# Loading the first tile in two DMAs of every other partition

## The chip, the core and the metric

The kernel runs on one core of one Trainium2 chip. The metric is the device time of one execution in microseconds (us). VectorE, ScalarE and GpSimd compute, SyncE only issues DMAs, and 16 DMA engines move the data between HBM and the core's on-chip memory of 128 partitions. TensorE is not used.

## What is computed

A mixture-of-experts combine. For each of 16 x 1024 tokens there are two expert rows of 512 float32 values and two weights; the output is the weighted sum of the two rows.

```python
weights = combine_weights[..., np.newaxis]
return np.sum(expert_outputs * weights, axis=2).astype(np.float32)
```

A token comes in as 4,096 bytes (two rows of 2,048) and goes out as 2,048. In all 67.2 MB are read and 33.6 MB written.

## The kernel before, in words

The 16,384 tokens are laid over the 128 partitions, 128 tokens to a partition. The first 115 tokens of a partition are neighbours in HBM, and the last 13 of each are taken from the end of the array (`rows`, L45). So a tile of 13 tokens is, for each partition, one contiguous row of 13 x 4,096 = 53,248 bytes ("52 KB").

There are ten tiles of 12 or 13 tokens (`TILES`, L32). They pass through four rooms in one buffer `et` (`ROOM`, `SITE`, L29 to L31): tile g uses room g modulo 4, so a room can be loaded again only when the output of the tile before in it has been stored. The results are written over the inputs, into the first half of the room, and stored from there.

Work on a tile (`combine`, L81): for tiles 0 to 7 VectorE multiplies the whole tile by the weights, spread along the rows (L88), and adds the two halves (L97). In tile 8, ScalarE shares the multiplications (L92, L94, L96). Tile 9 goes token by token, ScalarE multiplying (L102) and VectorE multiplying and adding (L103). All weights lie in one buffer `wt`.

The order is written out by hand (`manual_schedule`, from L107):

- ScalarE's queue (q10 in the profile) first issues a small store of a zero tile, 16 rows of 512 bytes (L111, overwritten later), then the weights of the first nine tiles, 128 rows of 920 bytes (L79), then the weights of the last tile in two halves of 64 partitions, rows of 104 bytes (L114). Later it issues the stores of tiles 0 to 6 (L130).
- SyncE's queue (q1) issues the loads of the first four tiles (L76). The first tile is loaded as 2 tokens, and these in packets of 4,096 bytes (`max_dma_last_dim`), and then 11 tokens in rows of 45,056 bytes (`FIRST`, L33). Each later load waits for the store that frees its room. The last two stores, tiles 7 and 8 together and tile 9, go out on this queue as well (L130).

There are nine DMAs before the first result: four on ScalarE's queue and five on SyncE's. The fifth load, that of tile 3, also waits until the small store of L111 has landed.

Of the kernel before, what the change touches and what calls it, by code (L numbers as in the profile page):

```python
# [1 line left out]

# [4 lines left out]


@with_exitstack
def kernel(  # L10
    ctx: ExitStack,
    tc: tile.TileContext,
    expert_outputs: bass.AP,
    combine_weights: bass.AP,
    out: bass.AP,
):

    nc = tc.nc
    b, s, k, h = expert_outputs.shape
    assert k == 2
    n = b * s
    P = nc.NUM_PARTITIONS
    per = n // P
    assert per * P == n

    ROOM = [13, 13, 12, 13]  # L29
    ROOMS = len(ROOM)  # L30
    SITE = [sum(ROOM[:i]) for i in range(ROOMS)]  # L31
    TILES = [13, 13, 12, 13, 13, 13, 12, 13, 13, 13]  # L32
    FIRST = [2, 11, 13, 12, 13]  # L33
    STORES = [[0], [1], [2], [3], [4], [5], [6], [7, 8], [9]]
    WHOLE = [0, 1, 2, 3, 4, 5, 6, 7]
    MIXED = [8]
    ALONE = 3
    FREE = {9: 0}
    LAST = 13
    assert all(c <= ROOM[g % ROOMS] for g, c in enumerate(TILES))  # L40
    assert sum(TILES) == per and [g for st in STORES for g in st] == list(range(len(TILES)))
    main = per - LAST
    starts = [sum(TILES[:g]) for g in range(len(TILES))]

    def rows(x):  # L45

        first = x[0 : P * main, :].rearrange("(p t) f -> p t f", p=P)
        second = x[P * main : n, :].rearrange("(p t) f -> p t f", p=P)
        return lambda t, c: first[:, t : t + c, :] if t < main else second[:, t - main : t - main + c, :]

    flat = out.rearrange("b s h -> (b s) h")
    eo = rows(expert_outputs.rearrange("b s k h -> (b s) (k h)"))
    cw = rows(combine_weights.rearrange("b s k -> (b s) k"))
    o = rows(flat)

    dt = mybir.dt.float32
    mult = mybir.AluOpType.mult
    add = mybir.AluOpType.add
    copy = mybir.ActivationFunctionType.Copy

    pool = ctx.enter_context(tc.tile_pool(name="all", bufs=1))
    et = pool.tile([P, sum(ROOM), k * h], dt)
    halves = et.rearrange("p j (k h) -> p (j k) h", k=k)
    wt = pool.tile([P, per * k], dt)
    wk = wt.rearrange("p (t k) -> p t k", k=k)
    zt = pool.tile([16, 128], dt)
    warm = pool.tile([P, 1], dt)

    def place(t):
        g = max(g for g in range(len(TILES)) if starts[g] <= t)  # L70
        return SITE[g % ROOMS] + t - starts[g]

    def load(t, c, **kw):
        at = place(t)
        assert place(t + c - 1) == at + c - 1
        nc.sync.dma_start(out=et[:, at : at + c], in_=eo(t, c), **kw)  # L76

    def weights(q, t, c):
        q.dma_start(out=wk[:, t : t + c, :], in_=cw(t, c))  # L79

    def combine(g, base):  # L81
        at, c, t0 = SITE[g % ROOMS], TILES[g], starts[g]
        if g in WHOLE or g in MIXED:
            room = halves[:, k * at : k * (at + c), :]
            x0, x1 = et[:, at : at + c, 0:h], et[:, at : at + c, h : 2 * h]
            if g in WHOLE:
                wb = wt[:, k * t0 : k * (t0 + c)].unsqueeze(2).to_broadcast([P, k * c, h])
                nc.vector.tensor_tensor(out=room, in0=room, in1=wb, op=mult)  # L88
            else:
                for i in range(ALONE, c):  # L90
                    x = et[:, at + i, 0:h]
                    nc.scalar.activation(out=x, in_=x, func=copy, scale=wt[:, k * (t0 + i) : k * (t0 + i) + 1])  # L92
                w1 = wk[:, t0 : t0 + c, 1:2].to_broadcast([P, c, h])
                nc.vector.tensor_tensor(out=x1, in0=x1, in1=w1, op=mult)  # L94
                w0 = wk[:, t0 : t0 + ALONE, 0:1].to_broadcast([P, ALONE, h])
                nc.vector.tensor_tensor(out=x0[:, 0:ALONE], in0=x0[:, 0:ALONE], in1=w0, op=mult)  # L96
            nc.vector.tensor_tensor(out=halves[:, base : base + c, :], in0=x0, in1=x1, op=add)  # L97
            return
        for i in range(c):
            t = k * (t0 + i)  # L100
            x0, x1 = halves[:, k * (at + i), :], halves[:, k * (at + i) + 1, :]
            nc.scalar.activation(out=x0, in_=x0, func=copy, scale=wt[:, t : t + 1])  # L102
            nc.vector.scalar_tensor_tensor(  # L103
                out=halves[:, base + i, :], in0=x1, scalar=wt[:, t + 1 : t + 2], in1=x0, op0=mult, op1=add
            )

    with tc.manual_schedule():  # L107
        nc.vector.memset(zt, 0.0)  # L108

        ahead = flat[0 : P * main, :].rearrange("(q t) h -> q (t h)", q=16)  # L110
        nc.scalar.dma_start(out=ahead[:, 0:128], in_=zt)  # L111
        weights(nc.scalar, 0, main)
        for half in (slice(0, P // 2), slice(P // 2, P)):
            nc.scalar.dma_start(out=wk[half, main:per, :], in_=cw(main, per - main)[half])  # L114
        nc.scalar.activation(out=warm, in_=nc.const_aps.tensor(1.0, (P, 1), dt), func=copy)  # L115

        t = 0
        for i, c in enumerate(FIRST):
            load(t, c, **({"max_dma_last_dim": k * h * 4} if i == 0 else {}))
            t += c  # L120
        assert t == sum(TILES[:ROOMS])
        for j, st in enumerate(STORES):
            room = FREE.get(st[0], st[0] % ROOMS)
            base, c = SITE[room] * k, 0
            for g in st:
                combine(g, base + c)
                c += TILES[g]
            assert c <= k * ROOM[room]
            q = nc.sync if j in (7, 8) else nc.scalar
            q.dma_start(out=o(starts[st[0]], c), in_=halves[:, base : base + c, :])  # L130
            for g in st:
                if g + ROOMS < len(TILES):
                    load(starts[g + ROOMS], TILES[g + ROOMS])


# [1 line left out]
_INS = ['expert_outputs', 'combine_weights']  # L137
_OUTS = [((16, 1024, 512), 'float32')]


# [23 lines left out]
```

## Time and profile before

| what | value |
|---|---|
| time, median of 3 runs | 238.83 us (238.82 to 238.92) |
| span of the profiled execution, first to last instruction | 237.1 us |
| time of the profiled execution itself | not recorded beside its span |
| VectorE busy | 190.0 us, 80% |
| ScalarE busy | 15.8 us, 7% |
| read from HBM, written to it | 67.24 MB, 33.56 MB |
| rate over the span | 425 GB/s |

The span counts from the first to the last instruction of one execution; the time also holds what lies before and after. A DMA queue's row gives packets, MB and the time that its packets took as a share of 16 engines over the span or window. "Landing" is the moment when a transfer's completion is signalled. A row of the timeline has start, duration, engine, line and operation, and in brackets the idle time before it with what ended it. In the chain of waits, each step is what released the next.

### The profile page before, as it was taken

What the parts mean: (1) busy time and instruction counts of PE and PEld (TensorE: products, weight loads), DVE (VectorE), ACT (ScalarE), POOL (GpSimd) and SP (SyncE); (2) the same over time, 40 slices, a digit from 0 to 9 for tenths busy, and PEclk for the clock granted to TensorE, in tenths of its full rate; (3) what the DMA queues carried; (4) which work ended last, traced back from release to release, by engine and by line L of the source; (5) the groups of instructions that cost most, each with busy time, mean ns of one, the idle gap of its engine ahead of it and who ended that gap; (6) DMA issues with size and microseconds to landing.
All of it is one profiled execution on the core that took longest, in us unless ns stands there. A gap on an engine that the chain in (4) does not pass through costs nothing.

```text
span 237.1 us, 154 instructions
## 1 busy us (share of the span) xinstructions
DVE 190.0 (80%) x33; ACT 15.8 (7%) x25; POOL 0.2 (0%) x4
## 2 busy tenths in 40 slices
DVE  0006999999999999999999998998499969919400
ACT  2000000000000000000000000000000055019200
POOL 0000000000000000000000000000000000000000
DMA  8999999989999999999899999999899999899996
GB/s 300 388 481 434 432 421 398 470 348 485 449 431 458 431 440 390 486 420 420 359 492 409 409 509 392 431 503 431 359 431 503 420 397 483 381 431 431 431 431 287
DMA packets 3344, 100.80 MB, mean 425 GB/s; under 512 B 512, under 2 KB 656, under 8 KB 912
## 3 DMA queue, kind: packets, MB, share of 16 engines
q1 hardware_dynamic: 2000, 77.33, 75.9%
q10 hardware_dynamic: 1344, 23.47, 23.0%
HBM read 67.24 MB, written 33.56 MB: 425 GB/s over the span
## 4 chain that ended last, share of the span: by engine, by line
DVE 55%; DMA 36%; issue 1%; ACT 0%; DVEq 0%; ACTq 0%; SPq 0%
DVE et L88 35%; DVE et L97 17%; DMA out_dram<-et 17%; DMA et<-in_expert_outputs_dram 12%; DMA wt<-in_combine_weights_dram 8%; DVE et L103 3%; ACT et L102 0%; DVEq L159 0%; ACTq L111 0%; DVE zt L108 0%; DVEq L88 0%; SPq L76 0%; ACTq L102 0%
## 5 line engine op out<-in xcount | busy, mean ns | idle before, releaser
L88 DVE TENSOR_TENSOR et<-et,wt 128x13312 f32<-128x13312 f32 (+1 forms) x8 | 110.0, 13754 | 23.8 <-DMA wt<-in_combine_weights_dram 18.7
L97 DVE TENSOR_TENSOR et<-et 128x6656 f32<-128x6656 f32 (+1 forms) x9 | 62.8, 6973 | 0.4
L92 ACT ACTIVATE et<-et,wt 128x512 f32<-128x512 f32 x10 | 6.2, 708 | 188.0 <-DMA et<-in_expert_outputs_dram 188.0
L103 DVE SCALAR_TENSOR_TENSOR et<-et,wt 128x512 f32<-128x512 f32 x13 | 8.7, 747 | 5.0 <-ACT et L102 5.0
L102 ACT ACTIVATE et<-et,wt 128x512 f32<-128x512 f32 x13 | 8.1, 707 | 14.0 <-DMA et<-in_expert_outputs_dram 14.0
L94 DVE TENSOR_TENSOR et<-et,wt 128x6656 f32<-128x6656 f32 x1 | 7.1, 7093 | 2.3 <-DMA et<-in_expert_outputs_dram 2.3
L96 DVE TENSOR_TENSOR et<-et,wt 128x1536 f32<-128x1536 f32 x1 | 1.8, 1751 | 0.0
L115 ACT ACT_TABLE_LOAD x1 | 1.3, 1283 | 3.1 <-issue 3.1
L108 DVE MEMSET zt<- 16x128 f32 x1 | 0.2, 165 | 0.8 <-PEq L148 0.8
L115 ACT ACTIVATE warm<-const-float32-1.0 128x1 f32<-128x1 f32 x1 | 0.2, 203 | 0.0
L148 POOL MEMSET const-bfloat16-1.0<- 128x1 bf16 x1 | 0.1, 102 | 0.0
L148 POOL MEMSET const-uint8-127<- 128x1 uint8 x1 | 0.1, 101 | 0.0
L148 POOL MEMSET const-float32-0.0<- 128x1 f32 x1 | 0.1, 99 | 0.2 <-issue 0.2
L148 POOL MEMSET const-float32-1.0<- 128x1 f32 x1 | 0.1, 98 | 0.0
## 6 DMA issues: line engine op xcount, KB each, us to landing
et<-in_expert_outputs_dram SPq DMA_DIRECT2D x7, 6656.0 KB, 32.2
out_dram<-et ACTq DMA_DIRECT2D x5, 3328.0 KB, 34.7
et<-in_expert_outputs_dram SPq DMA_DIRECT2D x2, 6144.0 KB, 41.1
out_dram<-et SPq DMA_DIRECT2D x1, 6656.0 KB, 19.9
out_dram<-et ACTq DMA_DIRECT2D x2, 3072.0 KB, 37.2
et<-in_expert_outputs_dram SPq DMA_DIRECT2D x1, 5632.0 KB, 18.2
out_dram<-et SPq DMA_DIRECT2D x1, 3328.0 KB, 14.0
et<-in_expert_outputs_dram SPq DMA_DIRECT2D x1, 1024.0 KB, 5.0
```

The costliest lines, as they stand in the source:

```text
L88: nc.vector.tensor_tensor(out=room, in0=room, in1=wb, op=mult)
L92: nc.scalar.activation(out=x, in_=x, func=copy, scale=wt[:, k * (t0 + i) : k * (t0 + i) + 1])
L94: nc.vector.tensor_tensor(out=x1, in0=x1, in1=w1, op=mult)
L96: nc.vector.tensor_tensor(out=x0[:, 0:ALONE], in0=x0[:, 0:ALONE], in1=w0, op=mult)
L97: nc.vector.tensor_tensor(out=halves[:, base : base + c, :], in0=x0, in1=x1, op=add)
L102: nc.scalar.activation(out=x0, in_=x0, func=copy, scale=wt[:, t : t + 1])
L103: nc.vector.scalar_tensor_tensor(out=halves[:, base + i, :], in0=x1, scalar=wt[:, t + 1 : t + 2], in1=x0, op0=mult, op1=add)
L108: nc.vector.memset(zt, 0.0)
L115: nc.scalar.activation(out=warm, in_=nc.const_aps.tensor(1.0, (P, 1), dt), func=copy)
L148: nc = _bacc.Bacc("TRN2", target_bir_lowering=False, num_devices=1)
```

## The change

The first tile (13 tokens, room 0) is loaded by two DMAs of 64 partitions each. The first takes partitions 0, 2, 4 ... 126, the second 1, 3, 5 ... 127. Each moves 64 rows of 53,248 bytes. Before, there were two DMAs as well: 2 tokens of all 128 partitions, then the other 11 tokens of all partitions. The other loads, the stores, the weights and the arithmetic stay as they are, and the number of DMAs is the same.

```diff
-    FIRST = [2, 11, 13, 12, 13]
+    FIRST = [13, 13, 12, 13]
...
-    def load(t, c, **kw):
+    def load(t, c):
         at = place(t)
         assert place(t + c - 1) == at + c - 1
-        nc.sync.dma_start(out=et[:, at : at + c], in_=eo(t, c), **kw)
+        nc.sync.dma_start(out=et[:, at : at + c], in_=eo(t, c))
...
-        t = 0
-        for i, c in enumerate(FIRST):
-            load(t, c, **({"max_dma_last_dim": k * h * 4} if i == 0 else {}))
+        for own in (slice(0, P, 2), slice(1, P, 2)):
+            nc.sync.dma_start(out=et[own, 0 : FIRST[0]], in_=eo(0, FIRST[0])[own])
+        t = FIRST[0]
+        for c in FIRST[1:]:
+            load(t, c)
             t += c
```

## Prediction

> **What bounds the kernel now.** I read the page first, its busy shares and its DMA parts.
>
> ```profile
> span 237.1 us, 154 instructions
> DVE 190.0 (80%) x33; ACT 15.8 (7%) x25; POOL 0.2 (0%) x4
> ...
> DMA  8999999989999999999899999999899999899996
> ...
> q1 hardware_dynamic: 2000, 77.33, 75.9%
> q10 hardware_dynamic: 1344, 23.47, 23.0%
> ```
>
> VectorE works 80% of the span. The DMA engines work 75.9 + 23.0 = 98.9% of it, which leaves 2.6 us of idle time on each. q1 is SyncE's queue (all loads, the last two stores), q10 is ScalarE's (weights, the other stores). The next question is where those 2.6 us lie, so I cut the span into stages with the windows view (columns: length, VectorE, ScalarE, GpSimd, clock, DMA share, GB/s).
>
> ```profile
> 0.00:1.80 1.80, 0.17 (x1) 0.00 (x0) 0.20 (x4) 1.00 0.00 0
> 1.80:5.20 3.40, 0.00 (x0) 1.49 (x2) 0.00 (x0) 1.00 1.18 404
> 5.20:18.70 13.50, 0.00 (x0) 0.00 (x0) 0.00 (x0) 1.00 0.98 424
> 18.70:34.50 15.80, 14.74 (x2) 0.00 (x0) 0.00 (x0) 1.00 1.00 432
> ...
> 52.00:145.00 93.00, 92.41 (x10) 0.00 (x0) 0.00 (x0) 1.00 1.00 434
> 145.00:212.40 67.40, 56.49 (x7) 6.23 (x10) 0.00 (x0) 1.00 1.02 440
> ...
> 236.30:237.10 0.80, 0.00 (x0) 0.00 (x0) 0.00 (x0) 1.00 0.00 0
> ```
>
> They lie at the two ends: 1.80 us before the first byte and 0.80 us after the last. Between them the engines never rest, so **the end is the start of the first transfer plus all DMA work**. Is VectorE anywhere as late as the DMA? The chain of waits and the timeline answer (start, duration, what; in brackets the idle time before).
>
> ```profile
> 1.43 18.21 DMA wt<-in_combine_weights_dram
> ...
> 144.62 39.25 DMA out_dram<-et
> 183.87 0.02 SPq L76
> 183.89 0.03 issue
> 183.92 28.80 DMA et<-in_expert_outputs_dram
> ```
>
> ```profile
> 19.73 14.02 DVE L88 TENSOR_TENSOR et<-et,wt 128x13312 f32<-128x13312 f32 x1 [18.75 <-DMA wt<-in_combine_weights_dram]
> ...
> 145.69 12.96 DVE L88 TENSOR_TENSOR et<-et,wt 128x12288 f32<-128x12288 f32 x1 [1.10 <-DMA et<-in_expert_outputs_dram]
> ...
> 169.18 14.03 DVE L88 TENSOR_TENSOR et<-et,wt 128x13312 f32<-128x13312 f32 x1 [3.94 <-DMA et<-in_expert_outputs_dram]
> ...
> 192.63 7.09 DVE L94 TENSOR_TENSOR et<-et,wt 128x6656 f32<-128x6656 f32 x1 [2.30 <-DMA et<-in_expert_outputs_dram]
> ```
>
> VectorE starts at 19.73, held by the weights (landed at 1.43 + 18.21 = 19.64), runs without a gap to 144.6, and from then on waits for loads: 1.10 + 3.94 + 2.30 = 7.34 us. So a start that is later by up to 7 us is given back before tile 8, as long as the queues stay filled; a DMA that is later is not.
>
> **What one row costs.** The second tile's load lies alone in 18.7 to 34.5, beside crumbs of weights. The queues in that window (packets, MB, share of 16 engines):
>
> ```profile
> q1 hardware_dynamic: 144, 6.80, 99.5%
> q10 hardware_dynamic: 143, 0.02, 0.8%
> ```
>
> 144 packets are 128 rows and 16 completion marks: a row of 53,248 B is one packet, and each of the 16 engines has eight. A row takes 15.8 x 0.995 / 8 = 1.965 us, 27.1 GB/s for an engine. The crumbs are the two transfers of L114, 64 rows of 104 B each. In the 0.45 us from 20.50, when each engine passes from one row to the next, the same view has:
>
> ```profile
> q1 hardware_dynamic: 16, 0.85, 436.9%
> q10 hardware_dynamic: 16, 0.00, 2.9%
> ```
>
> Sixteen rows of 53,248 B (0.85 MB), and sixteen of the 104 B packets between them. Two things follow. The queues take turns, a packet of q1, a packet of q10. And **a transfer of 64 rows is dealt to all 16 engines, four rows each**: the first of these halves covers partitions 0 to 63 alone, and yet every engine has a packet of it. [...]
>
> **The change, part by part.** DMA times of the first tile and the weights, from the view of DMA issues (count, KB, us from issue to landing), and SyncE's first issue:
>
> ```profile
> et<-in_expert_outputs_dram SPq DMA_DIRECT2D x1, 5632.0 KB, 18.2
> ...
> et<-in_expert_outputs_dram SPq DMA_DIRECT2D x1, 1024.0 KB, 5.0
> wt<-in_combine_weights_dram ACTq DMA_DIRECT2D x1, 115.0 KB, 18.2
> ```
>
> ```profile
> 0.73 0.44 SPq L76 DMA_DIRECT2D et<-in_expert_outputs_dram  x1
> ```
>
> 1. Issues. Two DMAs go, two come, on the same queue and in the same place, so the number of issues and what the later loads wait for do not change. The first takes 0.44 us; the new one, with fewer packets, costs between 0 and 0.44. I take 0.44, no gain; the other end would let everything start 0.4 us earlier.
>
> 2. Packets. Per engine 16 packets of 4,096 B and 8 of 45,056 B become 8 of 53,248 B. What the first ones took is seen in the queue's row for 0 to 5.2 us:
>
> ```profile
> q1 hardware_dynamic: 272, 1.36, 76.5%
> ```
>
> 1.36 MB are the 256 packets of 4,096 B (1.05 MB) and the first seven long rows (0.32 MB), so the 2 tokens were through at about 5.1. Their 64 KB per engine need 65,536 / 27.1 = 2.4 us and took 3.3 from the first byte at 1.80: 0.8 to 0.9 us are lost at the start. Whether long rows lose as much isn't shown: between nothing (a gain of 0.8) and one loss of that size for each of the two DMAs (0.8 more). The nearest row is this start, so I take 0.8 again. The sixteen packets that go cost something apiece: the 143 crumbs above, hardly any bytes, took 0.8% of 16 x 15.8 us, 14 ns each. That bounds it at 0.2 us, and I take 0.1.
>
> 3. The rate of the new rows is the term that decides, and no row of before shows a bulk transfer of 64 rows. From below, a row takes 1.965 us as in the second tile: nothing changes. From above: if the four rows of an engine are dealt in order, engine 0 writes partitions 0, 2, 4, 6, the next 8 to 14, and so on. [...] Eight rows cost 8 x 1.965 = 15.7 us more. [...] I take 3.93.
>
> [...]
>
> 4. The weights. Now their 8 packets alternate with the 8 rows of 45,056 B and land with the tile (18.2 us after issue both, the rows issued at about 1.2). Ahead of them on q10 stands the small store of L111 with its mark. In the new order these two also need gaps between rows, and the gaps are 2 us apart instead of 0.15 (4,096 B at 27.1 GB/s). Row 1, store; row 2, mark; then eight weights, then their mark: eleven turns of q10, against eight rows and two marks on q1. So the weights land at least one row of the second tile after the first tile, and up to three if the store is queued a row or two later: 2 to 6 us. VectorE is held that much longer; the 7.34 us of later waits cover it, and the DMA works on the second tile meanwhile. Cost nothing; beyond 7 us each us would count.
>
> **Sum.** Row term +15.7, packets -0.1, and a small gain where one engine of a pair runs ahead of the other by some tenths of a us and has the next group for itself, at most 0.8, taken as 0.2: **+15.4 us**. The tile lands at about 19.4 + 15.5 = 35, the weights a row later at 37, VectorE starts at 37.2 instead of 19.73. All later loads and stores move by the same 15.5, since the engines stay filled, and the 2 us that VectorE loses beyond that go into its waits. Span 237.1 + 15.4 = 252.5. The median shown is 238.83, 1.7 us above the span, for what lies around it (the profiled execution's own time is not given beside it); with the same 1.7, 254.2.
>
> **The rivals.**
>
> *Unpaired (not slower): 238.7.* If the four rows of each engine lie so that engines keep apart, a row stays at 1.965 us; what decides is whether two engines meet, and anything up to 1.97 us a row gives this case. [...] Then only the packets count, -0.1 us, and the start, 0.4 either way: 238.3 to 239.1. The late weights are hidden, as above.
>
> *A quicker start: 238.0.* As the last one, but long rows hide the loss at the start, and the shorter issue lets the first byte come earlier: 0.1 + 0.5 + 0.2 = 0.8 us less. For it: nothing is due between the first byte and the second tile but bytes. [...]
>
> *Half a meeting: 240 to 252.* Engines meet in a part of their rows (one of the two DMAs, or one row in two): +7.8 us, 246.6. Nothing in the trace speaks for it.
>
> **How the numbers follow.** Paired 0.56, unpaired 0.32, a quicker start 0.07, half a meeting 0.05. The likeliest gives the time, **254.2**, with a range of its own of 252.8 (0.8 gained by engines out of step, 0.4 at the issue, some at the start) to 255.0 (one more loss at the start). Paired alone doesn't hold 8 in 10, so the range reaches to the unpaired case: 238.2 to 255.0. By over 0.2% (0.48 us, about what can be told from no change) faster: 0.07. Within: 0.31 of the unpaired. Slower: 0.56 + 0.05 + 0.01 = 0.62.
>
> **What would show it.** In the changed kernel's windows, 1.8 to 34 at some 215 GB/s says paired; 430 from 3 us on says unpaired. The first tile's DMAs should land near 19 and 35 (unpaired: near 11 and 19), the weights one to three rows behind; VectorE's first start at 37 (21 to 25). In all cases the DMA share from the second tile on should stay near 1.00, and VectorE's waits at 145 and 169 should shrink by what the weights cost. The prediction is wrong if a row of the first tile takes 1.97 us, or if the late weights open a gap in the DMA that the rest doesn't close.

## The result, and the profile after

The changed kernel takes 241.14 us (median of 6 runs, 239.93 to 241.50) against 238.85 us before, a ratio of 1.0092 [1.0075, 1.0108]: 2.3 us slower, where 15.4 were forecast. The span of the profiled execution is 239.7 us in place of 237.1. From the page of the changed kernel, the lines that the prediction showed of the page before:

```profile
span 239.7 us, 154 instructions
DVE 190.0 (79%) x33; ACT 15.8 (7%) x25; POOL 0.2 (0%) x4
...
DMA  7999999999999999899999999999999999999993
...
q1 hardware_dynamic: 1744, 77.33, 75.1%
q10 hardware_dynamic: 1344, 23.47, 22.8%
```

The bytes are the same, and the DMA row is full to the last slice but one. Its windows (length, VectorE, ScalarE, GpSimd, clock, DMA share, GB/s):

```profile
1.80:2.00 0.20, 0.00 (x0) 0.00 (x0) 0.00 (x0) 1.00 0.00 0
2.00:3.20 1.20, 0.00 (x0) 0.00 (x0) 0.00 (x0) 1.00 2.01 666
3.20:4.00 0.80, 0.00 (x0) 0.40 (x1) 0.00 (x0) 1.00 0.17 67
6.00:18.40 12.40, 0.00 (x0) 0.00 (x0) 0.00 (x0) 1.00 0.97 419
```

419 GB/s from 6 to 18.4 us: no engine held up another, the rows of the first tile took 1.97 us each. What is new stands above it. The first byte moves after 2.00 us, not 1.80. A packet's bytes are booked where it starts: 666 GB/s over 1.2 us are 15 rows of 53,248 B, and the 67 GB/s of 3.20 to 4.00 are one row. Fifteen engines begin by 3.2 us; **the sixteenth begins after it** (at 3.50 in the packet records). It is still the last one tile later. At the start of the second tile, the queues' rows of two windows, 18.60 to 19.45 and 19.45 to 20.50:

```profile
q1 hardware_dynamic: 29, 0.80, 217.8%
q10 hardware_dynamic: 28, 0.03, 8.6%
```

```profile
q1 hardware_dynamic: 2, 0.05, 11.8%
q10 hardware_dynamic: 2, 0.00, 0.5%
```

0.80 MB are fifteen rows, and the sixteenth (0.05 MB) begins alone, at 19.76. And at the end of the run, changed kernel first, before second:

```profile
235.80:236.60 0.80, 0.00 (x0) 0.00 (x0) 0.00 (x0) 1.00 0.09 33
236.60:237.60 1.00, 0.00 (x0) 0.00 (x0) 0.00 (x0) 1.00 0.06 27
```

```profile
234.00:235.00 1.00, 0.00 (x0) 0.00 (x0) 0.00 (x0) 1.00 1.05 453
235.00:236.00 1.00, 0.00 (x0) 0.00 (x0) 0.00 (x0) 1.00 0.01 0
```

Before, the last packets of all 16 engines start within one window and then nothing is left. After, two more windows pass in which 33 and 27 GB/s move: one packet of 26,624 B each. **One engine is 2 us behind, and the run ends when it ends.** The packet records give the numbers: when each engine begins the third tile's load, and when it ends its last packet. (A record names no engine; a packet is counted to the engine whose packet before ended where this one starts. The "middle engine" is the median of the sixteen.) The middle engine begins the third tile at 34.82 in place of 34.60 and ends at 236.30 in place of 235.74, +0.56. The last engine is 0.72 us behind the middle one at the third tile and 2.25 at the end; before, 0.14 and 0.24. So of the 2.6 us in the profile, 0.56 are lost by all and 2.0 by one.

That one engine begins late is not new. Before, the last engine begins its first load packet at 2.64 and the middle one at 1.90, 0.74 us apart, and yet it is level with the others at the third tile. In all 17 traces of this case the last engine begins its loads 0.5 to 1.4 us after the middle one. What differs is whether an engine is still behind at the third tile.

VectorE's side, the timeline of the changed kernel:

```profile
22.19 14.03 DVE L88 TENSOR_TENSOR et<-et,wt 128x13312 f32<-128x13312 f32 x1 [21.21 <-DMA wt<-in_combine_weights_dram]
...
147.24 12.96 DVE L88 TENSOR_TENSOR et<-et,wt 128x12288 f32<-128x12288 f32 x1 [0.20 <-DMA et<-in_expert_outputs_dram]
...
170.76 14.02 DVE L88 TENSOR_TENSOR et<-et,wt 128x13312 f32<-128x13312 f32 x1 [3.97 <-DMA et<-in_expert_outputs_dram]
...
194.26 7.09 DVE L94 TENSOR_TENSOR et<-et,wt 128x6656 f32<-128x6656 f32 x1 [2.35 <-DMA et<-in_expert_outputs_dram]
```

It starts 2.46 us later, behind the weights, as forecast for the unpaired case. But its later waits shrink only from 7.34 to 6.52 us in all: the loads that it waits for come later as well (the tile of 169.18 now starts at 170.76), which fits loads that end with their last engine.

### The profile page after: what moved, and what is told of

Same layout as the page of the kernel before. It is cut to its first block, busy times and chain, and to the rows that moved or that the text cites. A ratio compares the mean times of both kernels' runs of the same rounds, so it can differ in the third digit from the quotient of the medians.

```text
span 239.7 us, 154 instructions
## 1 busy us (share of the span) xinstructions
DVE 190.0 (79%) x33; ACT 15.8 (7%) x25; POOL 0.2 (0%) x4
## 4 chain that ended last, share of the span: by engine, by line
DVE 54%; DMA 37%; issue 2%; ACT 0%; DVEq 0%; ACTq 0%; SPq 0%
DVE et L88 35%; DMA out_dram<-et 17%; DVE et L97 16%; DMA et<-in_expert_outputs_dram 11%; DMA wt<-in_combine_weights_dram 9%; DVE et L103 3%; ACT et L102 0%; DVEq L161 0%; ACTq L111 0%; DVE zt L108 0%; DVEq L88 0%; SPq L76 0%; ACTq L102 0%
```

## The experiments

Three theories were put at first. **A**: an engine that begins its first long row late stays behind, and long first rows cause it. **B**: the split by even and odd partitions does the harm. **C**: VectorE's late start does. "Lag" below is that of the last engine behind the middle one, at the third tile's start and at the end, from the packet records of the profiled execution. Each kernel has one such trace, so a lag is that of one execution. The kernel before, run again beside the experiments, took over 239.1 us once in 79 runs (240.89).

**Halves of neighbouring partitions (e4)**, for the step on which the forecast stood.

```diff
-for own in (slice(0, P, 2), slice(1, P, 2)):
+for own in (slice(0, P // 2), slice(P // 2, P)):
```

> Halves of partitions 0 to 63 and 64 to 127 in place of even and odd, rows of 53,248 B. If engines meet in pairs on neighbouring partitions, as the prediction held for even and odd: a row of the first tile takes 3.93 us, the tile lands near 35, 254 to 256 us. If they do not meet here either: 239.9 to 241.5, as the changed kernel (theory A), or 238.8 to 239.2 if only the even and odd split does harm (theory B).

255.80 us, ratio 1.0706 [1.0690, 1.0722]. Windows of this kernel:

```profile
6.00:18.00 12.00, 0.00 (x0) 0.00 (x0) 0.00 (x0) 1.00 0.91 188
18.00:34.00 16.00, 0.00 (x0) 0.00 (x0) 0.00 (x0) 1.00 1.05 218
36.00:52.00 16.00, 13.13 (x1) 0.00 (x0) 0.00 (x0) 1.00 0.97 417
```

For 28 us the engines are "busy" and move half of what they move afterwards. So the 64 rows of one half of the partitions move at half the rate (188 and 218 GB/s against 417), at about the price that the prediction gave for engines that meet: the middle engine begins the third tile at 51.77, 16.95 us later than in the changed kernel. Every other partition doesn't bring them together (419 GB/s). The rows of partitions 0 to 63 also lie in one half of the part of HBM that the tile is read from, so this run alone doesn't show on which side the engines meet.

**The whole tile in one DMA (e1).**

```diff
-for own in (slice(0, P, 2), slice(1, P, 2)):
-    nc.sync.dma_start(out=et[own, 0 : FIRST[0]], in_=eo(0, FIRST[0])[own])
+nc.sync.dma_start(out=et[:, 0 : FIRST[0]], in_=eo(0, FIRST[0]))
```

> First tile in one DMA of 128 rows of 53,248 B, no split. Theory A (an engine that begins its first long row late stays behind to the end; the size of the first packets decides): as the changed kernel, 239.9 to 241.5 us, one engine 1 to 2.5 us behind the others at the end. Theory B (the split by even and odd partitions does the harm): as before, 238.8 to 239.2. Theory C (the late start of VectorE does it): the weights land one row later than in the changed kernel, so 241 to 243. The small number of DMAs (four loads ahead, not five) also frees the fourth load from its wait for the small store.

242.59 us, ratio 1.0174 [1.0141, 1.0207]; lag 0.78 and 1.93. An engine is late without any split, which speaks against B alone. The weights land at 25.7 and VectorE starts at 25.82. The middle engine ends at 237.50, 1.2 us later than in the changed kernel. Two things are seen here that the changed kernel does not have: engines stand idle near 82 and 214 us (0.28 us each on average), and the rows that begin between 80 and 91 us take 0.98 us per engine longer in all. That much theory C could claim, at 3.6 us more of delay; why those rows are slow isn't known.

**Even and odd in short packets (e2)**: `max_dma_last_dim=k * h * 4` added to both DMAs.

> Even and odd partitions as in the changed kernel, but in packets of 4,096 B. Theory A: no engine falls behind, so near before plus 0.5 us for 80 more packets per engine: 238.9 to 239.5. Theory B: still 239.9 to 241.5. Theory C: the weights find their gaps early and land with the tile or before, so as theory A.

240.25 us, ratio 1.0057 [1.0042, 1.0072]. The third tile begins 1.2 us later than before, for 80 more packets per engine and a first byte at 2.19; one engine lags by 0.77, and by the same 0.77 at the end. The time lies where theory B had it, but no theory expected a lag that doesn't grow.

**The first load in packets of 8,192 B (e3)**: before, without `max_dma_last_dim`.

> The kernel before without its limit of 4,096 B on the first load: 2 tokens in packets of 8,192 B, then 11. Theory A (packet size at the start): 8,192 B is far nearer to 4,096 than to 53,248, so 238.8 to 239.2. Theory B: 238.8. Theory C: the weights lose a few early gaps and land one row of 1.7 us later, so 239 to 240.

238.85 us, ratio 0.9990 [0.9973, 1.0006]; lag 0.29 and 0.23. As theories A and B have it, and not C.

**VectorE late, start as before (e5).**

```diff
 nc.scalar.dma_start(out=ahead[:, 0:128], in_=zt)
+nc.scalar.dma_start(out=wk[slice(0, 16), main:per, :], in_=cw(main, per - main)[slice(0, 16)])
 weights(nc.scalar, 0, main)
-for half in (slice(0, P // 2), slice(P // 2, P)):
-    nc.scalar.dma_start(out=wk[half, main:per, :], in_=cw(main, per - main)[half])
+nc.scalar.dma_start(out=wk[slice(16, P), main:per, :], in_=cw(main, per - main)[slice(16, P)])
```

> The kernel before, first tile as it was (2 tokens in short packets, then 11), but 16 rows of the last tile's weights go ahead of the main weights on ScalarE's queue, two more turns, so the weights should land some 4 us later and VectorE start near 23.5. Theory A (the start of the DMA engines decides, VectorE's start doesn't matter): 238.8 to 239.2, all engines ending within 0.5 us of each other. Theory C (the late start of VectorE costs): 240.5 to 242.5.

239.40 us, ratio 1.0022 [1.0013, 1.0031], lag 0.15 and 0.36. Its timeline:

```profile
23.42 14.03 DVE L88 TENSOR_TENSOR et<-et,wt 128x13312 f32<-128x13312 f32 x1 [22.45 <-DMA wt<-in_combine_weights_dram]
...
168.82 14.02 DVE L88 TENSOR_TENSOR et<-et,wt 128x13312 f32<-128x13312 f32 x1 [1.07 <-DMA et<-in_expert_outputs_dram]
```

3.7 us of delay cost 0.5 us; the rest came out of the later waits (none at 145 us, 1.07 instead of 3.94 at 169). Most of the 0.5 is seen in the rows of the third tile that are under way when the first store begins to move data (49.6 us here, 45.8 before): they take 0.76 us longer than the others on average, before 0.39.

**Weights early in the changed kernel (e6)**: the weights issued ahead of the small store.

> The changed kernel with the weights issued ahead of the small store of L111, so that they need two turns fewer and land with the first tile, VectorE starting near 20 in place of 22.2. Theory A: no help, 239.9 to 241.5, the last engine still 1 to 2.5 us behind. Theory C: 238.9 to 239.5.

240.91 us, ratio 1.0082 [1.0067, 1.0097]. Timeline and the end of the run:

```profile
20.03 14.03 DVE L88 TENSOR_TENSOR et<-et,wt 128x13312 f32<-128x13312 f32 x1 [19.05 <-DMA et<-in_expert_outputs_dram]
```

```profile
235.00:236.00 1.00, 0.00 (x0) 0.00 (x0) 0.00 (x0) 1.00 0.19 80
236.00:237.00 1.00, 0.00 (x0) 0.00 (x0) 0.00 (x0) 1.00 0.06 27
237.00:238.00 1.00, 0.00 (x0) 0.00 (x0) 0.00 (x0) 1.00 0.06 27
```

Lag 0.75 and 2.21. VectorE starts 2.2 us earlier, now held by the tile and not by the weights, which land 2.1 us after their issue. The middle engine ends at 235.79, as before the change (235.74), and one engine still ends 2.21 us behind it. **That engine alone makes about 2 of the 2.3 us**; theory C is out for them.

**2 tokens first, then even and odd (e8)**, with `FIRST` as before the change.

```diff
 weights(nc.scalar, 0, main)
-for half in (slice(0, P // 2), slice(P // 2, P)):
-    nc.scalar.dma_start(out=wk[half, main:per, :], in_=cw(main, per - main)[half])
+weights(nc.scalar, main, per - main)
...
 for i, c in enumerate(FIRST):
-    load(t, c, **({"max_dma_last_dim": k * h * 4} if i == 0 else {}))
+    if i == 1:
+        for own in (slice(0, P, 2), slice(1, P, 2)):
+            nc.sync.dma_start(out=et[own, t : t + c], in_=eo(t, c)[own])
+    else:
+        load(t, c, **({"max_dma_last_dim": k * h * 4} if i == 0 else {}))
```

> 2 tokens of all partitions in packets of 4,096 B first, as before, then the other 11 tokens in even and odd partitions, rows of 45,056 B (the two halves of the last weights in one DMA, so that the number of DMAs stays nine). Theory A (only long rows as the first packets put engines out of step): 238.8 to 239.2. Theory B in its remaining form (64-row transfers themselves cost, in the issue or in the dealing): 239.5 to 241.5. Weights: one more mark on the load queue gives them a turn more, so they land with the tile and theory C expects 238.9.

238.91 us, ratio 1.0010 [0.9995, 1.0026], lag 0.16 and 0.19, and from 235 to 236 us no data moves any more:

```profile
5.20:18.70 13.50, 0.00 (x0) 0.00 (x0) 0.00 (x0) 1.00 0.97 419
234.00:235.00 1.00, 0.00 (x0) 0.00 (x0) 0.00 (x0) 1.00 0.99 426
235.00:236.00 1.00, 0.00 (x0) 0.00 (x0) 0.00 (x0) 1.00 0.01 0
```

One of its ten runs took 240.72; that one was not traced. In the median the split into even and odd costs nothing behind the 2 tokens. What costs is that it comes first (after against e8).

**Order exchanged (e9)**: `load(2, 11)`, then `load(0, 2)` in short packets, all partitions.

> The two DMAs of the first tile as before (11 tokens in rows of 45,056 B, 2 tokens in packets of 4,096 B, all 128 partitions), with only their order exchanged. Theory A (the first packets of the program must not be long rows): 240 to 242, one engine 1 to 2.5 us behind the others at the end, as in the changed kernel. If it needs the 64-row form, or another number or size of packets: 238.8 to 239.3. The weights find many gaps among the short packets at the tile's end, so VectorE should start near 20 and theory C expects 239.

239.76 us, ratio 1.0040 [1.0027, 1.0054], lag 0.46 and 0.69. A miss for theory A as I had put it: long rows first, and no engine 2 us behind in this trace (its run took 239.55; the ten runs reach from 239.27 to 240.98). Two engines lost 0.9 and 1.2 us near the first store.

**The changed kernel once more (e10).**

> The changed kernel once more, for a second trace. Theory A: again one engine (of 16) 1 to 2.5 us behind at the end and 0.4 to 1 us behind at the start of the second tile, 239.9 to 241.5. If the late engine of the first trace was an accident: all engines end within 0.5 us, 239 to 239.5.

One run, 241.22 us; lag 0.77 and 2.08. At the end a second engine is 1.13 us behind and a third 0.54. The late engine was no accident of one trace.

**1 token, then 12 (e11).**

> The kernel before with 1 token in packets of 4,096 B and then 12, in place of 2 and 11: half as many short packets ahead of the long rows. Theory A: 238.7 to 239.2 if eight short packets are enough to take up the slow start, 239.5 to 241 with an engine behind if they are not. The weights land about one row of 1.8 us later than before; by the late weights of the run before that costs at most 0.3 us.

238.87 us, ratio 0.9998 [0.9988, 1.0008]; but one of its 11 runs took 240.82, and it is the one that was profiled (span 239.0). Its trace shows why: lag 0.61 and 2.16.

```profile
235.00:236.00 1.00, 0.00 (x0) 0.00 (x0) 0.00 (x0) 1.00 0.07 27
236.00:237.00 1.00, 0.00 (x0) 0.00 (x0) 0.00 (x0) 1.00 0.06 27
```

Here the late engine looks like a matter of chance, though none of the ten quick runs was traced. With the change it is there in both executions that were traced, but one of the six runs took only 239.93.

**One half long, one short (e12, e13)**: short packets for the odd or for the even partitions alone. Theory A2 was new: short packets let engines draw level again, wherever they stand.

> The changed kernel with its second DMA (odd partitions) in packets of 4,096 B; the first, of even partitions, stays in rows of 53,248 B. Theory A2 (long rows keep the lag that engines have, short packets behind them take it up before the second tile): engines within 0.4 us at the second tile's start, none 1 us or more behind at the end, 239.0 to 239.8. Theory A as first put (the first packets must not be long): one engine behind, 240 to 242.

> The other way round: even partitions in packets of 4,096 B, odd in rows of 53,248 B. Theory A and A2 alike: the short packets take up the slow start, 239.0 to 239.8, no engine behind. If 64-row transfers leave an engine late whatever their packets, as the run with short packets for both halves hinted (one engine 0.5 us behind): 240 to 241.5.

e12: 240.89 us, 1.0073 [1.0049, 1.0097], lag 0.71 and 2.00. e13: 241.31 us, 1.0099 [1.0084, 1.0114], lag 0.67 and 2.17. Both refute A2, and e13 refutes A: its first packets are short, and an engine is late all the same, as its third case had it.

**What about the start makes an engine late (e14, e15, e16)**: 2 tokens by even and odd, short packets, then 11 of all; the whole tile of 128 rows in short packets; 6 tokens in short packets, then 7.

> The kernel before with its first load (2 tokens, packets of 4,096 B) split into even and odd partitions, the 11 tokens in one DMA of all partitions as before; the halves of the last weights in one DMA, to keep nine. Theory S (the 64-row form at the start leaves one engine late): 240 to 241.5, last engine 0.6 us or more behind the middle at the third tile's start, 2 us at the end. Theory R (what counts is that every engine soon reads from all its partitions): 238.8 to 239.3, lag under 0.4.

> First tile in one DMA of 128 rows, packets of 4,096 B, each engine going through the 13 tokens of a partition before the next. Theory S: lag under 0.4, 239.3 to 239.9 (80 packets more per engine, some 0.6 us, and no late engine). Theory R: an engine 0.6 us late at the third tile, 240.3 to 242.

> 6 tokens of all partitions in packets of 4,096 B, then 7. If the number of short packets sets how close the engines come: lag as before or less, 238.9 to 239.3 (32 packets more, 0.2 to 0.3 us). Theory R: the first partition of an engine is left after 1 us in place of 0.3, so a late engine in some executions, median 239 to 240.

e14: 240.70 us, 1.0064 [1.0035, 1.0094], lag 0.89 and 1.43; its six runs fall into two groups, 239.3 (two runs) and 240.6 to 241.3 (four). The end of its trace, where three engines are behind:

```profile
236.00:237.00 1.00, 0.00 (x0) 0.00 (x0) 0.00 (x0) 1.00 0.19 80
237.00:238.00 1.00, 0.00 (x0) 0.00 (x0) 0.00 (x0) 1.00 0.00 0
```

e15: 239.96 us, 1.0047 [1.0030, 1.0063], lag 0.58 and 0.53. e16: 239.09 us, 1.0023 [1.0003, 1.0043], lag 0.20 and 0.21, with two of ten runs near 240.9. So the 64-row form at the start is enough to leave an engine behind, in most runs, even with 2 tokens and short packets (e14 differs from before only in this and in the last weights as one DMA, which e8 has too), and 128 rows in short packets leave less lag (e15, e16). Long rows of 128 partitions (e1) leave an engine behind too. Neither theory had e15 right: its time lies just above the range of S, its lag just below that of R. e16 fits both of its cases in the median, and R in its two late runs.

All traces together show a pattern in this kernel, with its limit drawn afterwards and 0.58 and 0.61 on its two sides. With a lag of 0.60 us or more at the third tile (after, e1, e6, e10, e11, e12, e13, e14) the last engine ends 1.4 to 2.3 us behind; with 0.58 or less (before, e3, e4, e5, e8, e9, e15, e16) 0.2 to 0.7. e2 alone has 0.77 and keeps it. Part of the growth lies in the rows of the third tile under way at the first store, where the late engine loses more than the others (in the changed kernel 0.91 us on its row of 46.4, against 0.48 on average). The rest, in three traces followed row by row, lies in the late engine's rows of the fourth tile: in the changed kernel 0.31 us on the row of 54.0, 0.51 on 60.2 and 0.25 on 69.6, in e10 0.23, 0.62 and 0.19 at 53.8, 60.0 and 69.4, in e11 0.26, 0.51 and 0.29 at 54.5, 60.7 and 69.1. In e6 it is the other way: 0.95 of its 1.46 us come ahead of the fourth tile.

**What stays open**: why one engine begins late in every kernel, why it (or another) is still behind at the third tile in some, what slows the rows of the late engine there, and why not in e2. No kernel here beats the one before: e3 and e11 (0.9990 and 0.9998) can't be told from it.

## Why the prediction was wrong, point by point

- **What bounds the kernel: right.** The DMA engines are never idle between start and end in the traces before and after (busy for 98.9% and 97.9% of the span), and the run ends behind their last packet. (In e1 they rest for 0.28 us each.) What was missed is that "the DMA engines" are sixteen. The sum was made for the mean; the end is that of the slowest, and a DMA share of 0.99 does not show an engine that trails.
- **Step 1, issues: wrong by a little.** A cost of no more than 0.44 us was taken for the first issue, because it has fewer packets; it took 0.55. SyncE's first two issues took 1.18 us in place of 0.95, and the first byte came at 2.04 in place of 1.81 (e3, with its plain load of 128 rows: 1.74). Before and after:

```profile
0.73 0.95 SPq L76 DMA_DIRECT2D et<-in_expert_outputs_dram  x2
```

```profile
0.73 1.18 SPq L118 DMA_DIRECT2D et<-in_expert_outputs_dram  x2
```

- **Step 2, packets and start: right for the middle engine** (third tile +0.22, as much as the first byte is later), wrong for the last, which begins its first row 1.3 us after the middle one and is still 0.72 behind at the third tile. A start loss was in the sum as one size for all engines; 2.0 of the 2.3 us come from one engine that the sum put at nothing.
- **Step 3, the rate: wrong, and this is the step that failed.** The term of +15.7 us stood for engines that meet in pairs and hold each other up, so that a row takes twice 1.965 us: "I take 3.93". It was the author's estimate, and so was the 0.2 us to be gained within a pair; no run shows either for even and odd partitions. Measured: 1.97 us a row, so the term is nothing. e4 shows that 64 rows can move at half the rate, at about the price given (16.95 us against 15.7), when they lie in one half of the partitions. The nearest row of before, 16 crumbs of a 64-row transfer, showed that all engines share 64 rows. It did not show which rows each gets, nor that two engines on different partitions ever hold each other up; the meeting in pairs needed both. No run shows how the rows are dealt, so which of the two was wrong stays open. The unpaired case at 0.32 had this step right: engines kept apart.
- **Step 4, the weights: right.** They landed at 1.43 + 20.68 = 22.11, about one row after the tile, as the count of turns gave:

```profile
1.43 20.68 DMA wt<-in_combine_weights_dram
```

  "Cost nothing" was nearly so: 3.7 us cost 0.5 in e5. For the 2.46 us here no run shows the cost alone; in e6, with VectorE 2.2 us earlier and the weights moved ahead of the first row, the middle engine ends 0.51 earlier.
- **The rivals.** The range held the time only because it had to reach from the unpaired to the paired case, and slower came true for another reason than the one given: both are luck. The one case whose span holds 241, half a meeting (240 to 252, 0.05), has engines that meet in part of their rows, and none did. The unpaired case has the rate right (1.97 us a row) but ends at 239.1. The quicker start did not come: the first byte moved 0.76 us after the end of the first issue, before 0.64, and the middle engine lost as much at the start as before. That one engine could be left behind was not among the cases, though the prediction's own count, seven long rows begun by 5.2 us on sixteen engines, showed engines out of step.

## What to carry to other kernels

When a kernel is bound by DMA from end to end, look for its slowest engine: cut the last microseconds into windows, and a rate of one sixteenth (here 27 of 426 GB/s) is one engine that the others wait for. What comes first on the queues had a say here in how far apart the engines run, and with equal work afterwards an engine left behind hardly caught up (0.58 us became 0.53 in e15, 0.77 stayed 0.77 in e2), and often fell further back (0.72 became 2.25 with the change). A load of 2 tokens of all 128 partitions ahead of the long rows was worth 2 us in most runs (241.14 us with the change, 238.91 in e8). And before a transfer is cut by partitions, ask which partitions each DMA then writes: rows of every other one ran at the full rate here (419 GB/s), the lower and the upper half at 188 to 218 GB/s, which cost 17 us.

## What the runs showed of the hardware that was not expected

- Transfers of 64 rows to every other partition ran at 419 GB/s, as fast as 128 rows (417 to 424), those to 64 neighbouring partitions at 188 to 218.
- A lag of 0.6 us or more among engines at the third tile did not stay what it was: it became about 2 us in seven of nine traces, most of it between 44 and 72 us in the four that were followed row by row (after, e6, e10, e11).
- Rows of a load under way when the first store began to move data took longer than the others: by 0.39 us on average before the change, 0.48 after it, 0.76 in e5, and by nothing in e2, e4 and e15. Why isn't known.
- Issuing one of the 64-row DMAs first took SyncE 0.55 us, a 128-row DMA in long rows 0.38 (e1), and the first byte came at 2.04 and 1.75.
